# Down projection of a Strassen-like FFN: activation sums formed by the producer, w_down resident, last stores through GpSimd

## The chip, the cores and the metric

The kernel runs on one core of one Trainium2 chip. The metric is the device time in microseconds (us), median over several executions. A core has the engines TensorE (PE, matrix products; its weight loads are PEld), VectorE (DVE), ScalarE (ACT), GpSimd (POOL) and SyncE (SP, which here only issues DMAs). ACT and POOL can issue DMAs too. Each engine works through its own queue in order and waits on semaphores for the others.

## The reference, cut to what matters

One layer of an encoder on 1280 tokens (256 of a prompt, 1024 of a sample), model width 1024. The attention part is not touched by the change. The FFN is, with 2816 hidden columns:

```python
h2 = rmsnorm(x, ffn_norm_g)
x = x + (jax.nn.silu(h2 @ w_gate) * (h2 @ w_up)) @ w_down
return rmsnorm(x, final_norm_g)
```

All is float32.

## The kernel before

**Products.** A float32 product is made of three matmuls on operands split in a high and a low half: high x high, high x low, low x high (`mm3`, L104 to L107). The high half is a cast on ACT, the low half a subtraction on DVE or POOL.

**Seven products instead of eight.** Tokens fall in two halves T of 640, the hidden and output columns in two halves too, and each 2x2 block product is made of 7 products m of sums of blocks, in the order `SEQ2` = 3, 6, 1, 5, 2, 4, 7. Product 3 and product 4 take one block of the activations as they are; the other five take a sum or a difference of two.

**Gate and up.** A loop over 11 tile pairs fp (L950 on) makes gate (i = 0) and up (i = 1) for two tiles of 128 hidden columns: per product 2 x 12 matmuls of 128x320. POOL makes the sums of weight blocks (L866) and the low halves of the weights (L870), ACT the high halves (L869). Results are added from PSUM into the blocks `z` or `zB` (buffers of 2) by DVE (L930, L932), the first of them copied by ACT (L927). `finish` (L934 on) takes Silu of gate, multiplies up with it (L940, DVE) and stores the block of 320 KB to DRAM (`act_d`), on ACT's queue. Pair 0 is made in another order, while the sums S of the normalised input are still being made and split (L834 to L844).

**Down projection.** 77 steps (m, f), 7 products of 11 steps. A step takes one activation operand (128x640) and one operand of w_down (128x512), 15 matmuls of 128x512: five token tiles of 128, three each, into five PSUM banks `d`. `act_operand` (L1024 on) loads blocks back from DRAM, keeps them, and makes the sum of two (L1031; DVE for product 1, else POOL); `w_operand` (L1042 on) loads one or two tiles of w_down for every step and lets POOL add them (L1049). `split_f` makes the halves (ACT L1021, DVE L1022), in `ah` (3 buffers) and `wA` or `wB` (2 and 3). After the last step of a product, `put` (L1060 on) adds each bank into one or two rows of the residual x5, on DVE (L1065, L1067): 10 additions for products with two targets. Product 4 is followed by the final norm of five rows (`final`), product 7 by that of the other five (`final_half`), with output buffers taken from old activation slots. Operands are fetched two steps ahead.

**The order of the work.** A scheduler with a timeline of its own sets the order on PE, DVE, ACT and POOL. SP is in program order: it issues the loads of the gate and up weights, then, of the down stage, per step the activation block, the tiles of w_down and a row of x5.

Of the kernel before, what the change touches and what calls it, by code (L numbers as in the profile page):

```python
# [18 lines left out]
P = 128  # L19
# [20 lines left out]
def encoder_trunk(ctx: ExitStack, tc: tile.TileContext, x_tm, x_T, g_attn, w_c, w_v, w_qk,  # L40
# [10 lines left out]
    act_d = [tc.dram_tile([P, NTOK], F32, name=f"act_d{f}") for f in range(NF)]  # L51
# [864 lines left out]
    def product(C, seen, w, m, s, bank=None):  # L916
# [6 lines left out]
        for fi, T, sign in M_OUT[m]:  # L923
# [78 lines left out]
    halves = l5b.tile([P, 5], F32, name="halves")

    def slot(f, dt):
        return home[f].tile([P, 2, NQ], dt, name=f"a{f}")

    def act_block(b, f):
        T, n = int(b[0]) - 1, f + NH * (int(b[1]) - 1)
        if n not in act:
            act[n] = (slot(n, F32), set())  # L1010
        t, have = act[n]
        if T not in have:
            load(t[:, T], act_d[n][:, T * NQ:(T + 1) * NQ])
            have.add(T)
        return t[:, T]

    def split_f(o, raw, early):
        if early:
            split_w(o[:, 0], o[:, 1], raw)
        else:  # L1020
            nc.scalar.copy(out=o[:, 0], in_=raw)  # L1021
            nc.vector.tensor_sub(out=o[:, 1], in0=raw, in1=o[:, 0])  # L1022

    def act_operand(m, f):  # L1024
        src = [act_block(b, f) for b in A_OP[m] if isinstance(b, str)]
# [6 lines left out]
        if m == 7 and f >= NH - NLAST:  # L1032
            h = slot(f - (NH - NLAST), F32R)
        else:
            h = r5a.tile([P, 2, NQ], F32R, name="ah", bufs=3)
        split_f(h, raw, m == 3 and f == 0)
        return h

    nw = [0]

    def w_operand(m, f):
        raw = l5a.tile([P, 2, 512], F32, name="wd", bufs=3)  # L1042
        bs = [b for b in B_OP[m] if isinstance(b, str)]
        at = [f + NH * (int(b[0]) - 1) + NF * (int(b[1]) - 1) for b in bs]
        lo, n = min(at), len(at)
        load(raw[:, 0:n], w_down[lo:max(at) + 1:max(max(at) - lo, 1)].rearrange("n p d -> p n d"))
# [4 lines left out]
        if m == 7 and f == NH - 1:  # L1051
            w = slot(NH - 1, F32R)[:, :, 0:512]
        else:
            pl, nm, nb = (l5a, "wA", 2) if nw[0] % 5 < 2 else (l5b, "wB", 3)
            w = pl.tile([P, 2, 512], F32R, name=nm, bufs=nb)
        nw[0] += 1
        split_f(w, raw[:, 0], m == 3 and f == 0)
# [190 lines left out]
```

## Time and profile before

| | us |
|---|---|
| median of 3 runs | 1691.48 (1691.11 to 1692.06) |
| the profiled execution, device time | 1691.29 |
| its span in the profile | 1689.5 |
| PE busy | 1612.1 (95%) |
| DVE busy | 934.8 (55%) |
| POOL busy | 860.5 (51%) |
| ACT busy | 752.0 (45%) |

The span is the time from the first to the last instruction that the profile shows. The gate and up stage lies at about 837 to 1383.5 us (pair 0 to 896), the down projection from there to 1681.6. Shares are means over the span, so the table has to be read stage by stage. The granted TensorE clock is 0.991 of full speed in the mean.

### The profile page before, as it was taken

The page shows a single profiled execution, that of the slowest core. Times are in us where ns is not written, and L with a number is a line of the kernel's source. Part 1 is how long each engine was busy: PE and PEld are TensorE (multiplying, and loading weights), DVE is VectorE, ACT ScalarE, POOL GpSimd, SP SyncE. Part 2 cuts the span into 40 slices and gives each one's busy share as a digit, 9 for nine tenths or more (in the row PEclk, how much of TensorE's full clock was granted, in tenths as well). Part 3 has the DMA queues.
Part 4 walks back from the last instruction along what each step waited for, and adds up shares of the span by engine and source line. Part 5 has one row for each costly group of instructions (what it writes and reads, how often), then busy time and mean ns, then how long its engine had stood idle before and what let it go on. Part 6 is the DMA issues. An engine that isn't in the chain of part 4 may idle for free.

```text
span 1689.5 us, 26000 instructions
## 1 busy us (share of the span) xinstructions
PE 1612.1 (95%) x9601; PEld 1447.1 (86%) x9601; DVE 934.8 (55%) x1540; ACT 752.0 (45%) x1563; POOL 860.5 (51%) x914
## 2 busy tenths in 40 slices
PE   7999999998899999999989999999999999888998
PEld 7887899987798888888879999999999997666886
DVE  5753044545677677435583444443344447999665
ACT  5433154544677777534453333333333333233443
POOL 3441434353011119235386766666676666987344
PEclk9999999999999999999999999999999999999999
DMA  6635202143001012334241222121122249753354
GB/s 230 202 108 141 58 24 59 35 147 110 29 12 32 22 54 73 97 113 138 100 134 41 82 82 81 57 81 59 50 81 82 81 139 328 250 177 122 112 148 177
DMA packets 128144, 175.20 MB, mean 104 GB/s; under 512 B 35216, under 2 KB 66832, under 8 KB 128016
## 3 DMA queue, kind: packets, MB, share of 16 engines
q1 hardware_dynamic: 88080, 135.18, 25.1%
q10 hardware_dynamic: 39936, 38.35, 6.7%
q8 instruction: 76, 1.25, 0.3%
q14 instruction: 52, 0.43, 0.1%
HBM read 133.84 MB, written 39.65 MB: 103 GB/s over the span
## 4 chain that ended last, share of the span: by engine, by line
PE 75%; DVE 6%; issue 6%; DMA 5%; POOL 5%; ACT 3%; SPq 0%; ACTq 0%; POOLq 0%; DVEq 0%
PE M L107 10%; PE M L106 10%; PE M L105 10%; PE o L681 3%; PE tp L674 3%; PE d L107 3%; PE d L105 3%; PE d L106 3%; PE na_o L457 2%; PE po L105 2%; PE pj L105 2%; PE po L106 2%; PE po L107 2%; PE pj L107 2%; PE pj L106 2%
## 5 line engine op out<-in xcount | busy, mean ns | idle before, releaser
L105 PE MATMUL M<-S,wc 128*128 128x320 f32 x1056 | 325.9, 309 | 2.9 <-ACT wc L869 2.5
L107 PE MATMUL M<-S,wc 128*128 128x320 f32 x1056 | 324.5, 309 | 4.1 <-POOL wc L870 4.1
L106 PE MATMUL M<-S,wc 128*128 128x320 f32 x1056 | 326.4, 309 | 2.1 <-DVE S L840 2.0
L870 POOL TENSOR_TENSOR wc<-sum,wc 128x512 fp32r<-128x512 f32 x110 | 150.6, 1370 | 113.6 <-ACT wc L869 113.6
L105 PEld LDWEIGHTS M<-S,wc 128*128 128x128 f32 x1056 | 198.1, 188 | 4.2 <-ACT wc L869 3.2
L107 PEld LDWEIGHTS M<-S,wc 128*128 128x128 f32 x1056 | 197.6, 188 | 4.6 <-POOL wc L870 4.6
L106 PEld LDWEIGHTS M<-S,wc 128*128 128x128 f32 x1056 | 198.1, 188 | 3.2 <-DVE S L840 3.1
L866 POOL TENSOR_TENSOR sum<-A,A 128x512 f32<-128x512 f32 x110 | 159.1, 1455 | 9.4 <-DMA A<-in_w_gate_dram 3.1
L869 ACT CAST wc<-sum 128x512 fp32r<-128x512 f32 x110 | 68.3, 621 | 213.0 <-PE M L106 173.1
L930 DVE TENSOR_TENSOR z<-M,z 128x320 f32<-128x320 f32 x144 | 67.8, 486 | 118.2 <-PE M L107 84.5
L1049 POOL TENSOR_TENSOR wd<-wd 128x512 f32<-128x512 f32 x55 | 84.8, 1543 | 75.7 <-DMA wd<-in_w_down_dram 60.4
L930 DVE TENSOR_TENSOR zB<-M,zB 128x320 f32<-128x320 f32 x120 | 56.8, 487 | 108.5 <-PE M L107 74.7
L96 DVE TENSOR_TENSOR PT<-tp,PT 128x512 fp32r<-128x512 f32 (+1 forms) x144 | 93.0, 657 | 40.3 <-ACT PT L95 38.9
L694 POOL TENSOR_TENSOR ob<-ob 128x128 f32<-128x128 f32 x40 | 18.3, 457 | 180.0 <-ACT ob L691 179.9
L95 ACT CAST PT<-tp 128x512 fp32r<-128x512 f32 (+1 forms) x144 | 79.1, 564 | 44.0 <-PE tp L674 41.0
L666 DVE TENSOR_REDUCE mm<-S 128x1 f32<-128x1024 f32 (+1 forms) x80 | 84.9, 1061 | 14.1 <-PE S L107 12.6
L107 PE MATMUL d<-wB,ah 128*128 128x512 f32 x210 | 79.1, 406 | 9.8 <-DVE ah L1022 9.8
L870 POOL TENSOR_TENSOR wc<-A,wc 128x512 fp32r<-128x512 f32 x44 | 65.1, 1481 | 45.3 <-ACT wc L869 45.3
L106 PE MATMUL d<-wB,ah 128*128 128x512 f32 x210 | 83.9, 403 | 1.6 <-DVE wB L1022 1.6
L674 PE MATMUL tp<-ident,ex 128*128 128x128 f32 x544 | 79.7, 274 | 4.8 <-ACT ex L668 3.5
L105 PE MATMUL d<-wB,ah 128*128 128x512 f32 x210 | 83.6, 401 | 0.1
L681 PE MATMUL o<-PT,v 128*128 128x256 f32 x544 | 81.5, 288 | 1.6 <-ACT PT L95 1.4
(418 smaller groups left out, 4311.4 us busy)
## 6 DMA issues: line engine op xcount, KB each, us to landing
wd<-in_w_down_dram SPq DMA_DIRECT2D x55, 512.0 KB
a<-act_d SPq DMA_DIRECT2D x44, 320.0 KB
A<-in_w_gate_dram SPq DMA_DIRECT2D x52, 256.0 KB
A<-in_w_up_dram SPq DMA_DIRECT2D x52, 256.0 KB
x<-in_x_tm_dram SPq DMA_DIRECT2D x20, 512.0 KB
act_d<-z ACTq DMA_DIRECT2D x24, 320.0 KB
cT_d<-stg ACTq DMA_DIRECT2D x20, 320.0 KB
act_d<-zB ACTq DMA_DIRECT2D x20, 320.0 KB
```

Source lines behind the costliest of these rows:

```text
L95: i = nc.scalar.copy(out=hi, in_=ps)
L96: nc.vector.tensor_sub(out=lo, in0=ps, in1=hi)
L105: nc.tensor.matmul(out, lhsT=sh, rhs=mh, start=first, stop=False)
L106: nc.tensor.matmul(out, lhsT=sh, rhs=ml, start=False, stop=False)
L107: nc.tensor.matmul(out, lhsT=sl, rhs=mh, start=False, stop=last)
L666: nc.vector.reduce_max(out=nm[:, u:u + 1], in_=S, axis=AX.X, negate=True)
L674: nc.tensor.transpose(tp[:, j], ex[:, kt * P:(kt + 1) * P], ident)
L681: nc.tensor.matmul(oT, lhsT=vv, rhs=pt[s][g][:, j], start=kt == 0 and s == 0, stop=kt == nkt - 1 and s == 1)
L866: nc.gpsimd.tensor_tensor(out=raw, in0=A[a], in1=A[b], op=op)
L870: i1 = nc.gpsimd.tensor_tensor(out=lo, in0=raw, in1=hi, op=ALU.subtract)
L930: nc.vector.tensor_add(out=o, in0=ps, in1=o)
L1049: nc.gpsimd.tensor_tensor(out=raw[:, 0], in0=raw[:, i], in1=raw[:, 1 - i], op=B_OP[m][1])
```

## The change

`finish` now makes all seven activation operands of the pair while its blocks are in SBUF: two are blocks as they are, five are sums made by DVE (L964 of the new kernel), put over gate's old blocks or, for product 5, over a block of up. It stores seven arrays of 320 KB per pair instead of four, on ACT's queue, those of the last pair on POOL's (`store_p`). The down stage loads one ready array per step (`as`, 4 buffers). Each tile of w_down is loaded once, 11 times 512 KB and 22 times 256 KB, and stays in SBUF (`w0_f`, `w1_f`); DVE adds two of them where a product wants a sum (`ws`, L1065 of the new kernel, 2 buffers). The halves of a step go to `ah` and `w` (5 buffers each), loads are issued four steps ahead, and the output rows of `final` have 2 buffers. One early load of constants is issued after four memsets instead of before them.

```diff
+    def store_p(out, in_):
+        nc.gpsimd.dma_start(out=out, in_=in_)
...
     def finish(G, U, which, m, fp):
...
                 nc.vector.tensor_mul(out=U[:, fi, cs], in0=U[:, fi, cs], in1=G[:, fi, cs])
-                store(act_d[2 * fp + fi][:, cs], U[:, fi, cs])
+        if which == 0:
+            return
...
+        for n in AFTER.get(m, ()):
+            src = [block(U, b) for b in ACT_OP[n] if isinstance(b, str)]
+            out = src[0]
+            if len(src) == 2:
+                out = block(G, INTO[n]) if n in INTO else src[1]
+                nc.vector.tensor_tensor(out=out, in0=src[0], in1=src[1], op=ACT_OP[n][1])
+            (store_p if fp == NF // 2 - 1 else store)(act_d[n][fp], out)
...
-            if m in (1, 6):
-                raw = r5a.tile([P, NQ], F32, name="as", bufs=2)
-            eng = nc.vector if m == 1 else nc.gpsimd
-            eng.tensor_tensor(out=raw, in0=src[0], in1=src[1], op=A_OP[m][1])
...
+    def load_a(m, f):
+        araw[m, f] = r5b.tile([P, NQ], F32, name="as", bufs=4)
+        load(araw[m, f], act_d[m][f])
+
     def act_operand(m, f):
...
+        h = r5b.tile([P, 2, NQ], F32R, name="ah", bufs=5)
+        split_f(h, araw.pop((m, f)))
+        return h
+
+    def w_operand(m, f):
+        src = [wraw[b, f] for b in B_OP[m] if isinstance(b, str)]
         raw = src[0]
         if len(src) == 2:
...
-        if n == 2:
-            i = at.index(lo)
-            nc.gpsimd.tensor_tensor(out=raw[:, 0], in0=raw[:, i], in1=raw[:, 1 - i],
-                                    op=B_OP[m][1])
...
+            raw = r5b.tile([P, 512], F32, name="ws", bufs=2)
+            nc.vector.tensor_tensor(out=raw, in0=src[0], in1=src[1], op=B_OP[m][1])
+        w = l5w.tile([P, 2, 512], F32R, name="w", bufs=5)
+        split_f(w, raw)
         return w
...
-        yo = slot(NLAST + n % 5, F32).rearrange("p a b -> p (a b)")[:, 0:D]
...
+        yo = r5a.tile([P, D], F32, name="yo", bufs=2)
...
-    AHEAD = 2
+    AHEAD, LOADED = 2, 4
...
+    for step in steps[:LOADED]:
+        bring(*step)
     for step in steps[:AHEAD]:
         fetch(*step)
     for i, (m, f) in enumerate(steps):
+        if i + LOADED < len(steps):
+            bring(*steps[i + LOADED])
         if i + AHEAD < len(steps):
             fetch(*steps[i + AHEAD])
```

The order moves at three places. First DVE's queue where gate/up hands over to the down projection. Before (M0, M1 are gate/up products in PSUM, z_14403 and z_14402 up and gate of the last pair, `ah`, `wA`, `wB` halves of the down stage's operands):

```order
L930 TENSOR_TENSOR z_14403<-M0_14890,z_14403 128x320
L930 TENSOR_TENSOR z_14403<-M1_14904,z_14403 128x320
L940 TENSOR_TENSOR z_14403<-z_14403,z_14402 128x640
L1022 TENSOR_TENSOR ah_14969<-a1_14967,ah_14969 128x640
L1022 TENSOR_TENSOR wA_14975<-wd_14972,wA_14975 128x512
L1022 TENSOR_TENSOR ah_14980<-a2_14978,ah_14980 128x640
```

And now, at the same place (z_14538 and z_14537 are up and gate, L964 the activation sums, L1065 the sums of w, L1029 the low halves):

```order
L934 TENSOR_TENSOR z_14538<-M1_15041,z_14538 128x320
L1065 TENSOR_TENSOR ws_15116<-w1_0_15093 128x512
L951 TENSOR_TENSOR z_14538<-z_14538,z_14537 128x640
L1029 TENSOR_TENSOR w_15118<-ws_15116,w_15118 128x512
L964 TENSOR_TENSOR z_14537<-z_14538 128x640 x2
L964 TENSOR_TENSOR z_14538<-z_14538 128x640
L1029 TENSOR_TENSOR ah_15113<-as_15095,ah_15113 128x640
L1065 TENSOR_TENSOR ws_15124<-w1_1_15097 128x512
L1029 TENSOR_TENSOR ah_15121<-as_15099,ah_15121 128x640
L1065 TENSOR_TENSOR ws_15138<-w1_2_15101 128x512
L1029 TENSOR_TENSOR w_15126<-ws_15124,w_15126 128x512
L1029 TENSOR_TENSOR w_15140<-ws_15138,w_15140 128x512
```

A w sum now stands before the last product with gate, and three activation sums stand before the first low half of an activation; the halves of step 0 were made on POOL before and are not in DVE's queue there.

The second place is SP's queue from the first load of the down stage on. Before (`a` activation blocks, `wd` tiles of w_down, `x5` rows of the residual):

```order
L63 DMA a0_14956<-act_d0_62 128x640
L63 DMA wd_14961<-in_w_down_dram 128x2x512
L63 DMA a1_14967<-act_d1_63 128x640
L63 DMA wd_14972<-in_w_down_dram 128x2x512
L63 DMA a2_14978<-act_d2_64 128x640
L63 DMA wd_14983<-in_w_down_dram 128x2x512
L63 DMA x5_14989<-xm_d0_84 128x512
L63 DMA a3_15011<-act_d3_65 128x640
L63 DMA wd_15016<-in_w_down_dram 128x2x512
```

And now:

```order
L64 DMA w1_0_15093<-in_w_down_dram 128x2x512
L64 DMA as_15095<-act3_d0_84 128x640
L64 DMA w1_1_15097<-in_w_down_dram 128x2x512
L64 DMA as_15099<-act3_d1_85 128x640
L64 DMA w1_2_15101<-in_w_down_dram 128x2x512
L64 DMA as_15103<-act3_d2_86 128x640
L64 DMA x5_15105<-xm_d0_139 128x512
L64 DMA w1_3_15107<-in_w_down_dram 128x2x512
L64 DMA as_15109<-act3_d3_87 128x640
```

The row x5_15105 lies where the gate and up blocks were, so its load waits for the last pair's stores, which POOL issues now; the tile of w_down for step 3 is queued behind it.

The third place is DVE's queue at the end of product 3 (`d_...` are the PSUM banks, L1065 before and L1075 now the additions of `put`). Before:

```order
L1022 TENSOR_TENSOR ah_15240<-as_15238,ah_15240 128x640
L1022 TENSOR_TENSOR wA_15246<-wd_15243,wA_15246 128x512
L1022 TENSOR_TENSOR wB_15273<-wd_15270,wB_15273 128x512
L1065 TENSOR_TENSOR x5_14989<-d_14991,x5_14989 128x512
L1065 TENSOR_TENSOR x5_15134<-d_14991,x5_15134 128x512
L1022 TENSOR_TENSOR ah_15267<-as_15265,ah_15267 128x640
L1065 TENSOR_TENSOR x5_15022<-d_14992,x5_15022 128x512
```

And now:

```order
L1065 TENSOR_TENSOR ws_15429<-w0_1_15366,w1_1_15097 128x512
L1029 TENSOR_TENSOR ah_15398<-as_15341,ah_15398 128x640
L1075 TENSOR_TENSOR x5_15105<-d_15143,x5_15105 128x512
L1075 TENSOR_TENSOR x5_15225<-d_15143,x5_15225 128x512
...
L1065 TENSOR_TENSOR ws_15467<-w0_2_15393,w1_2_15101 128x512
L1029 TENSOR_TENSOR ah_15426<-as_15368,ah_15426 128x640
L1075 TENSOR_TENSOR x5_15167<-d_15146,x5_15167 128x512
...
L1075 TENSOR_TENSOR x5_15314<-d_15147,x5_15314 128x512
L1029 TENSOR_TENSOR w_15431<-ws_15429,w_15431 128x512
```

Before, both halves of w for the second step of product 6 (wB_15273) were made ahead of the additions; now its low half (w_15431) stands behind all ten.

## Rows read from the trace of the kernel before

**Rows 1.** Page: span; busy time, share of it and instructions of each engine.
```profile
span 1689.5 us, 26000 instructions
...
PE 1612.1 (95%) x9601; PEld 1447.1 (86%) x9601; DVE 934.8 (55%) x1540; ACT 752.0 (45%) x1563; POOL 860.5 (51%) x914
```

**Rows 2.** Stages: stretch, length, then PE, PEld, DVE, ACT, POOL busy, clock, DMA share, GB/s.
```profile
837.00:896.00 59.00, 48.88 (x318) 46.25 (x318) 47.58 (x59) 30.45 (x47) 45.44 (x27) 1.00 0.31 102
896.00:1383.50 487.50, 487.50 (x3327) 487.50 (x3327) 196.16 (x359) 170.65 (x332) 329.67 (x240) 1.00 0.21 72
1383.50:1430.00 46.50, 46.50 (x200) 36.72 (x199) 29.77 (x34) 16.85 (x27) 27.12 (x19) 1.00 0.93 338
1430.00:1550.00 120.00, 100.09 (x395) 73.60 (x394) 115.88 (x87) 36.83 (x58) 106.04 (x57) 0.97 0.57 195
1550.00:1681.60 131.60, 131.60 (x566) 105.92 (x564) 89.25 (x113) 56.83 (x100) 50.73 (x49) 1.00 0.44 138
```

**Rows 3.** PE in order of time: start, us, line, operation, tile.
```profile
1383.36 0.31 PE L107 MATMUL M<-zA,wc 128*128 128x320 f32 x1
1383.51 1.32 PE L105 MATMUL d<-wA,ah 128*128 128x512 f32 x5
...
1560.00 0.40 PE L105 MATMUL d<-wB,ah 128*128 128x512 f32 x1
...
1566.77 0.40 PE L107 MATMUL d<-wB,ah 128*128 128x512 f32 x1
...
1681.40 0.40 PE L107 MATMUL d<-a,a 128*128 128x512 f32 x1
```

**Rows 4.** Two stretches of 5 us, columns as in rows 2.
```profile
845.00:850.00 5.00, 2.73 (x15) 2.24 (x16) 2.82 (x4) 3.23 (x5) 5.00 (x4) 1.00 0.42 128
...
1470.00:1475.00 5.00, 3.89 (x11) 2.45 (x11) 5.00 (x4) 1.68 (x3) 5.00 (x4) 0.61 0.08 9
```

**Rows 5.** Waits, 1375 to 1690: who waits for whom, us, times, longest.
```profile
PEld d L107 <- DVE ah L1022: 26.9, 21, 2.6
```

**Rows 6.** DVE's groups by form, 1384 to 1410: count, busy us, mean ns, idle before.
```profile
L1022 DVE TENSOR_TENSOR ah<-a,ah 128x640 fp32r<-128x640 f32 x8 | 7.7, 958 | 3.0 <-ACT ah L1021 3.0
L1022 DVE TENSOR_TENSOR wB<-wd,wB 128x512 fp32r<-128x512 f32 x5 | 3.5, 691 | 7.8 <-ACT wB L1021 7.8
```

**Rows 7.** The same, 1440 to 1550.
```profile
L1022 DVE TENSOR_TENSOR ah<-as,ah 128x640 fp32r<-128x640 f32 x17 | 29.8, 1753 | 0.2 <-ACT ah L1021 0.2
...
L1065 DVE TENSOR_TENSOR x<-d,x 128x512 f32<-128x512 f32 x15 | 9.4, 675 | 0.0
```

**Rows 8.** POOL's groups by form, 1440 to 1550.
```profile
L1031 POOL TENSOR_TENSOR a<-a,a 128x640 f32<-128x640 f32 x22 | 44.9, 2041 | 4.9 <-DMA a<-act_d 4.8
L1049 POOL TENSOR_TENSOR wd<-wd 128x512 f32<-128x512 f32 x16 | 28.3, 1766 | 3.5 <-DMA wd<-in_w_down_dram 1.5 <-DVE as L1031 0.7 <-DVE wA L1022 0.7
```

**Rows 9.** DVE in order of time at the handover.
```profile
1384.23 0.82 DVE L940 TENSOR_TENSOR z<-z 128x640 f32<-128x640 f32 x1
1386.22 0.83 DVE L1022 TENSOR_TENSOR ah<-a,ah 128x640 fp32r<-128x640 f32 x1 [1.16 <-ACT ah L1021]
1386.96 0.68 DVE L1022 TENSOR_TENSOR wA<-wd,wA 128x512 fp32r<-128x512 f32 x1
```

**Rows 10.** Chain that ended last, 1375 to 1410: start, us, what.
```profile
1382.51 2.96 DMA act_d<-z
...
1386.45 5.03 DMA wd<-in_w_down_dram
```

**Rows 11.** DVE's groups by form, 1555 to 1660.
```profile
L1022 DVE TENSOR_TENSOR ah<-a,ah 128x640 fp32r<-128x640 f32 x29 | 28.2, 971 | 24.6 <-ACT ah L1021 24.6
...
L1076 DVE SCALAR_TENSOR_TENSOR a<-x,ry,gl_b 128x1024 f32<-128x1024 f32 x5 | 6.3, 1272 | 0.0
```

**Rows 12.** Weight loads in order of time, tile pair 0.
```profile
888.24 0.19 PEld L107 LDWEIGHTS M<-S,wc 128*128 128x128 f32 x1 [2.30 <-POOL wc L870]
```

**Rows 13.** DVE's and POOL's groups by form, 896 to 1383.
```profile
L940 DVE TENSOR_TENSOR z<-z 128x640 f32<-128x640 f32 x20 | 25.5, 1275 | 0.8
L866 POOL TENSOR_TENSOR sum<-A,A 128x512 f32<-128x512 f32 x97 | 133.8, 1388 | 5.5 <-POOL wc L870 0.8
```

More of the change, by code (lines that the diff above doesn't have):

```diff
@@ L50, in encoder_trunk @@
     rope_d = tc.dram_tile([2, 2, P, NTOK], F32R, name="rope_d")
-    act_d = [tc.dram_tile([P, NTOK], F32, name=f"act_d{f}") for f in range(NF)]
+    act_d = {m: [tc.dram_tile([P, NTOK // 2], F32, name=f"act{m}_d{f}") for f in range(NF // 2)]
+             for m in range(1, 8)}
     xm_d = [tc.dram_tile([P, D], F32, name=f"xm_d{t}") for t in range(NT)]
@@ L372, in encoder_trunk @@
             nc.gpsimd.memset(z[64 - 64 * hh:128 - 64 * hh].bitcast(F32), 0.0)
+    load(mp_s, m_prompt)
     def na_bias(p):
@@ L932, in product @@
                 nc.vector.tensor_sub(out=o, in0=o, in1=ps)
+    ACT_OP = {3: ("11",), 4: ("22",), 2: ("21", ALU.add, "22"), 7: ("12", ALU.subtract, "22"),
+              1: ("11", ALU.add, "22"), 6: ("21", ALU.subtract, "11"),
+              5: ("11", ALU.add, "12")}
+    AFTER = {2: (4, 2), 4: (7,), 7: (3, 1, 6, 5)}
+    INTO = {2: "21", 7: "12", 1: "22", 6: "11"}
     def finish(G, U, which, m, fp):
@@ L940, in finish, with block @@
                 nc.vector.tensor_mul(out=U[:, fi, cs], in0=U[:, fi, cs], in1=G[:, fi, cs])
-                store(act_d[2 * fp + fi][:, cs], U[:, fi, cs])
+        if which == 0:
+            return
+        def block(X, b):
+            T, fi = int(b[0]) - 1, int(b[1]) - 1
+            return X[:, fi, T * NQ:(T + 1) * NQ]
+        for n in AFTER.get(m, ()):
[5 more added lines that the diff above has]
+            (store_p if fp == NF // 2 - 1 else store)(act_d[n][fp], out)
     last = last + w31[1, 1][2:]
@@ L995, in encoder_trunk @@
     NLAST = 5
-    l5a, l5x, l5b = l5 = [pool("l5a"), pool("l5x"), pool("l5b")]
-    r5a, r5b, r5c, r5d = r5 = [pool(nm, side="right") for nm in ("r5a", "r5b", "r5c", "r5d")]
+    l5w, l5x, l5r = l5 = [pool("l5w"), pool("l5x"), pool("l5r")]
+    r5a, r5b = r5 = [pool(nm, side="right") for nm in ("r5a", "r5b")]
     pd = pool("pd", space=PSUM)
-    home = {f: r5c if f < 4 else r5d if f < 8 else l5b if f < 11 or f > 19 else r5b for f in range(NF)}
-    act, xs, ssy = {}, {}, {}
-    gl_b = l5b.tile([P, D], F32, name="gl_b")
@@ L1002, in encoder_trunk @@
[L1002 to L1022, printed above, removed]
@@ L1024, in act_operand, with split_f, load_w @@
-    def act_operand(m, f):
-        src = [act_block(b, f) for b in A_OP[m] if isinstance(b, str)]
+    xs, wraw = {}, {}
+    gl_b = r5a.tile([P, D], F32, name="gl_b")
+    halves = r5a.tile([P, 5], F32, name="halves")
+    def split_f(o, raw):
+        nc.scalar.copy(out=o[:, 0], in_=raw)
+        nc.vector.tensor_sub(out=o[:, 1], in0=raw, in1=o[:, 0])
+    def load_w(m, f):
+        bs = [b for b in B_OP[m] if isinstance(b, str) and (b, f) not in wraw]
+        if not bs:
+            return
+        dh = int(bs[0][1]) - 1
+        if ("t", dh, f) not in wraw:
+            pl = l5r if dh == 1 and f < NH - 1 else r5a
+            wraw["t", dh, f] = pl.tile([P, 2, 512], F32, name=f"w{dh}_{f}")
+        t = wraw["t", dh, f]
+        ks = sorted(int(b[0]) - 1 for b in bs if int(b[1]) - 1 == dh)
+        at = 2 * f + NF * dh
+        load(t[:, ks[0]:ks[-1] + 1],
+             w_down[at + ks[0]:at + ks[-1] + 1].rearrange("n p d -> p n d"))
+        for k in ks:
+            wraw[f"{k + 1}{dh + 1}", f] = t[:, k]
+        load_w(m, f)
@@ L1030, in act_operand @@
-            eng = nc.vector if m == 1 else nc.gpsimd
-            eng.tensor_tensor(out=raw, in0=src[0], in1=src[1], op=A_OP[m][1])
[L1032 to L1046, printed above, removed]
-        if n == 2:
-            i = at.index(lo)
-            nc.gpsimd.tensor_tensor(out=raw[:, 0], in0=raw[:, i], in1=raw[:, 1 - i],
-                                    op=B_OP[m][1])
[L1051 to L1057, printed above, removed]
@@ L1070, in final @@
         x = xs[n]
-        yo = slot(NLAST + n % 5, F32).rearrange("p a b -> p (a b)")[:, 0:D]
-        ss = l5b.tile([P, 1], F32, name="ssy", bufs=3)
-        r = l5b.tile([P, 1], F32, name="ry", bufs=3)
+        yo = r5a.tile([P, D], F32, name="yo", bufs=2)
+        ss = r5a.tile([P, 1], F32, name="ssy", bufs=3)
+        r = r5a.tile([P, 1], F32, name="ry", bufs=3)
         nc.scalar.activation(yo, x, AF.Square, accum_out=ss)
@@ L1087, in final_half @@
         x, half = xs[n], halves[:, n:n + 1]
-        yo = slot(NLAST + n % 5, F32).rearrange("p a b -> p (a b)")[:, 0:D]
-        ss = l5b.tile([P, 1], F32, name="ssy", bufs=3)
-        r = l5b.tile([P, 1], F32, name="ry", bufs=3)
+        yo = l5r.tile([P, 2, 512], F32, name=f"w1_{n}").rearrange("p a b -> p (a b)")
+        ss = r5a.tile([P, 1], F32, name="ssy", bufs=3)
+        r = r5a.tile([P, 1], F32, name="ry", bufs=3)
         nc.scalar.activation(yo[:, 0:512], x[:, 0:512], AF.Square, accum_out=ss)
@@ L1108, in fetch, with bring @@
         ops[m, f] = act_operand(m, f), w_operand(m, f)
+    def bring(m, f):
+        load_w(m, f)
+        load_a(m, f)
         for n in (f - 2,) if 2 <= f < NH - 1 else (NT - 2, NT - 1) if f == NH - 1 else ():
```

2 lines of the change are left out of this document (1 added, 1 removed).

## The prediction

> **What bounds the kernel now.** I read the page's busy times first, then a table of the span by stage, then the matmuls' pitch, then the waits of the slow stage, and last what VectorE (DVE) and GpSimd (POOL) do in it. TensorE (PE) is busy 95% of the span [rows 1], but that is an average over stages. In the gate/up stage after tile pair 0 (896 to 1383.5) PE is busy all 487.5 us: nothing can be gained there, only lost. In the down stage it is full from 1383.5 to 1430, busy 100.1 of 120 us from 1430 to 1550, full again to 1681.6, and the span ends at 1689.5, 7.9 us later [rows 1, 2].
>
> How much is lost in the down stage follows from the pitch. Between 1560.00 and 1566.77 there are 29 matmuls of 128x512 without a pause, 6.77/29 = 0.2334 us each. The stage has 7 products x 11 steps x 15 = 1155 of them, 1155 x 0.2334 = 269.6 us. It runs from 1383.51 to 1681.63 (the last one begins at 1681.40) [rows 3], 298.1 us. So 28.5 us are lost. The outer stretches are worth 46.5/0.2334 = 199 and 131.6/0.2334 = 564 matmuls, which leaves 392 in the middle, 91.5 us of work in 120 us: all 28.5 us are lost there. 19.9 of them are gaps; the rest is slow matmuls, among them 5 us at a mean granted clock of 0.61, so partly at 1.2 instead of 2.4 GHz, behind the gaps [rows 4].
>
> What PE waits for there is DVE's low half of the activation operand (26.9 us on the weight loads alone) [rows 5]. DVE is busy 115.9 of the 120 us and POOL 106.0 [rows 2]. Yet DVE's work is not long in itself: the low half of `ah` takes 958 ns and that of `wB` 691 from 1384 to 1410 [rows 6], and 1753 ns from 1440 to 1550 [rows 7], when POOL runs sums of 2041 and 1766 ns next to each other [rows 8]. PSUM additions, with one operand in SBUF, stay at 675 ns [rows 7]. So the two engines hold each other up where both read two SBUF operands, and PE pays. DMA load isn't it: DVE is at its short durations while DMA is at 0.93 share before 1430, and slow at 0.57.
>
> **The change part by part, down stage.** All of POOL's sums in this stage go; POOL is left with a few tiny operations and 5 multiplies. DVE gets the sums of w. Per step it then does a w sum, the low half of w (0.6 to 0.7 us each by the length at 1386.96 [rows 9]) and the low half of the activation (0.74 to 0.83 by spacing and length at 1386.22 [rows 9]), about 2.0 us; 60 additions from PSUM of 0.68 [rows 7] over 77 steps add 0.5. That is 2.6 us against PE's 15 x 0.2334 = 3.50 us per step, so PE sets the pace: I take back the whole 28.5 us, and then count what the new order gives away. Loads are no limit on average: in the first product 832 KB per step and 256 KB of x5 in 3.5 us are 311 GB/s, and 338 were moved over the stretch to 1430 with PE full [rows 2].
>
> *Handover.* Call T the end of the last gate/up matmul, 1383.36 + 0.31 = 1383.67 [rows 3]. Before, the first down operand was ready early (built by POOL) and PE went on without a gap. Now DVE's queue has the first w sum behind the last addition from PSUM, and then the product with gate, the low half of w, and three of the five activation sums, and only then the first activation's low half. By the durations there [rows 9]: addition done T+0.53 (the next operation starts at 1384.23); w sum T+1.14; ScalarE's high half T+1.8; product T+1.96; low half of w T+2.6; three sums (0.7 to 0.8) T+4.7; low half of the activation T+5.45. PE's first ten matmuls of step 0 fit before, the last five run from 5.45 to 6.7. Step 1: DVE does w sum (6.1), low half (6.8), w sum 2 (7.4), low half of w (8.0); the five first matmuls run from 6.7, the other ten from 8.0 to 10.4. Step 2 is ready by then and ends T+13.9. Three steps alone need 10.5: 3.4 us lost.
>
> *The stores through POOL.* The first x5 load stands in SP's queue behind nothing but waits for the last pair's stores (its space is the old gate and up tiles), and w1_3 stands behind it. The last of those stores is issued at about T+3.9. No store by POOL is in these rows; the nearest is ScalarE's of the same block, 2.96 us from issue to landing, and for the loads after it 5.03 us for 512 KB [rows 10]. With 4.7 us for the store, x5_0 goes at T+8.6, w1_3 lands near T+12.8, its sum, high half and first matmuls are at T+14.9 instead of 13.9: 1.0 us. With the 2.96 of the row it is 0; with a store twice as slow, 5 us more (rival 1).
>
> *First boundary.* At the end of product 3 each of 5 banks is added into two places, 10 additions, and in DVE's queue the low half of w for product 6, step 1 stands behind all ten, with a w sum and an activation's low half among them. The first bank is done 4 x 0.2334 = 0.93 us before the product's end: -0.93 + 10 x 0.61 (0.68 less an overlap as at 1386.22) + 0.65 + 0.75 + 0.65 gives 7.2 us after that end; PE, with step 0 and the first third of step 1 to do, comes to it at 3.5 + 1.17 = 4.67. 2.6 us lost. At the five other boundaries three steps (10.5 us) are prepared in front of the additions: 0.
>
> *Last product.* Output rows have 2 buffers instead of 5, so ScalarE's square waits for a store two rows back and holds the high halves queued behind it. The final row costs DVE 1272 ns and ScalarE about as much [rows 11]. By my count the operand of step 8 is ready at 24.5 us into the product, needed at 24.7: between 0 and 3, I take 0.5. The tail after the last matmul stays at 7.9 us.
>
> *Gate/up.* Five sums and three more stores per tile pair go on DVE and ScalarE, 11 times. In pair 0, DVE is the late one already (busy 47.6 of 59 us with PE at 48.9 [rows 2], and a weight load that waits 2.30 us for POOL's low half [rows 12]); one new sum of 0.82 stands ahead of the S7 split: 0.8, at most 3 sums, 2.5. In the ten others, operands are made three products ahead; POOL is 329.7/487.5 = 68% busy, DVE 40% [rows 2]: 0, with the cover being POOL's 16 us of idle time per pair of 48.9 us. The DVE product of the same shape takes 1275 ns there against 825 alone, because of POOL [rows 9, 13]. The extra 0.45 us is what meeting an operation of 1388 ns in 68% of cases would cost on average (0.68 x 0.69 = 0.47). The Trainium skill says of this (SBUF — State Buffer, "Who interferes with whom") that a DVE instruction with two SBUF inputs and a GpSimd instruction that reads SBUF exclude each other for a whole instruction, whoever starts first; the trace agrees by that 0.45. Blocked POOL time is then 5 x 0.83 = 4.2 us per pair, inside 16.
>
> Moving one early load behind four memsets changes no engine's order: 0.
>
> **Sum.** 1691.3 (the profiled execution: span 1689.5 and 1.8 around it, 0.2 under the median of 1691.48) - 28.5 + 3.4 + 1.0 + 2.6 + 0.5 + 0.8 = 1671.1. Nothing given away would be 1662.8. The same stalls could bring the lower clock back: 5 us at 0.61 cost 0.39 x 5 = 2 us, while a stretch with PE busy 2.73 of 5 us left it at 1.00 [rows 4]; I count none. Likeliest case alone: 1667 to 1677.
>
> **Rivals.**
> 1. *The stores through POOL are held up* while DVE works without pause at the handover. For it: DVE has about 13 us of queue with hardly a gap there, and both engines hold each other up in this trace. Against it: no store by POOL is shown. Price: x5_0 only when DVE first pauses, near T+13, w1_3 usable at T+19 instead of 14: 5 us, 1676. The Trainium skill has such a rule (SBUF — State Buffer, "SBUF: two separate sides"): GpSimd can't write a DMA's descriptors while VectorE holds the shared port. No row here shows it.
> 2. *DVE itself becomes the bound.* If its operations stay nearer the 971 ns that `ah` has from 1555 to 1660 [rows 11], each boundary stalls like the first: 5 x 2.6 = 13 more, 1684. Against it: in that stretch POOL still ran 50.7 of 131.6 us [rows 2]. With a stall in the last product on top, 1688 to 1691, no change.
> 3. *Slower: gate/up pays.* PE has no slack there. ScalarE issues the stores in order, behind the sums that they wait for, and makes the high halves of the weights. If that, with POOL blocked, makes PE wait over 20.2/11 = 1.8 us per pair, the gain is gone; two of the five sums uncovered, each with a blocked POOL operation (2 x 1.27), are 2.5 us x 11 = 28: 1699. Against it: PE waits nowhere there now, with operands six halves ahead.
>
> **How the numbers follow.** Likeliest 0.55; rival 1 0.13; rival 2 0.12, and its no-change form 0.05; rival 3 0.08; less given away (1663 to 1667) 0.07. Range 1664 to 1684. A measurement of this kernel tells about 0.2%, 3.4 us, from no change. Faster 0.55 + 0.13 + 0.12 + 0.07 = 0.87, same 0.05, slower 0.08.
>
> **What would show it.** In the profile after: 1430 to 1550 with PE above 95%, `ah` low halves near 0.8 us and POOL nearly idle; a gap of 3 to 5 us in the first 15 us of the down stage, PE waiting for DVE and then for w1_3; one near 2.6 us after product 3 and no other of its size; gate/up after pair 0 still 487.5 us. Wrong if `ah` stays at 1.7 us with POOL silent, if gate/up is longer by more than 5 us, or if PE waits at every boundary.

## The result and the profile after

The changed kernel takes 1668.97 us (median of 4 runs, 1667.90 to 1670.22) against 1691.77 us for the kernel before (4 runs). The ratio is 0.9864, with a 95% interval from 0.9847 to 0.9881: 1.4% faster. The forecast was 1671 us.

The page of the changed kernel, span and busy times:

```profile
span 1667.8 us, 26037 instructions
...
PE 1607.0 (96%) x9601; PEld 1450.4 (87%) x9601; DVE 950.5 (57%) x1641; ACT 751.4 (45%) x1565; POOL 689.2 (41%) x818
```

PE and DVE do about what they did before [rows 1]; POOL lost 171 us. A share of the span says little about where that helped, so next come the stages, with the same columns as [rows 2] (length, busy PE, PEld, DVE, ACT, POOL, clock, DMA share, GB/s):

```profile
837.00:896.00 59.00, 52.08 (x331) 49.76 (x330) 51.06 (x58) 29.65 (x45) 49.03 (x28) 0.97 0.33 110
896.00:1379.50 483.50, 483.50 (x3299) 483.27 (x3297) 249.16 (x407) 169.96 (x332) 318.88 (x235) 1.00 0.25 89
1379.50:1430.00 50.50, 44.37 (x186) 34.42 (x185) 35.90 (x54) 19.04 (x30) 2.53 (x5) 1.00 0.92 342
1430.00:1550.00 120.00, 119.05 (x502) 95.73 (x503) 78.98 (x117) 45.88 (x78) 5.25 (x5) 0.99 0.40 127
1550.00:1659.60 109.60, 109.60 (x470) 88.19 (x468) 78.28 (x112) 45.21 (x77) 11.79 (x21) 1.00 0.42 135
```

The stretch from 1430 to 1550, with PE busy 100.1 us before, is nearly full (119.05). POOL is silent there, and DVE fell from 115.9 to 79.0 us although it took the w sums over. In exchange the first 50 us of the down stage are no longer full: 44.4 of 50.5. The gate/up stage stayed full with 53 us more work on DVE.

PE in order of time, the starts behind a gap of the down stage, the last gate/up matmul and the last matmul of all (start, us, line, operation, tile, idle before and who ended it):

```profile
1379.23 0.31 PE L111 MATMUL M<-zA,wc 128*128 128x320 f32 x1
1381.99 0.50 PE L109 MATMUL d<-w,ah 128*128 128x512 f32 x1 [2.46 <-ACT ah L1028]
...
1385.03 1.43 PE L111 MATMUL d<-w,ah 128*128 128x512 f32 x5 [0.43 <-DVE ah L1029]
...
1395.40 1.44 PE L109 MATMUL d<-w,ah 128*128 128x512 f32 x5 [1.71 <-ACT ah L1028]
...
1430.95 0.50 PE L110 MATMUL d<-w,ah 128*128 128x512 f32 x1 [2.48 <-DVE w L1029]
...
1659.59 0.40 PE L111 MATMUL d<-w,ah 128*128 128x512 f32 x1
```

These four are the only gaps over 0.25 us in the 77 steps; before there were 20. I use one measure from here on: from the start of the last gate/up matmul to the start of the last down matmul. It was 1681.40 - 1383.36 = 298.04 us [rows 3] and is 1659.59 - 1379.23 = 280.36 us. The whole difference of the two profiled executions (spans 1689.51 and 1667.78, 21.73 us) is put together from the start times of single matmuls, which stand in the same order in both:

| stretch | before | after | difference | forecast |
|---|---|---|---|---|
| up to the first gate/up matmul | 800.94 | 798.10 | -2.84 | 0 |
| tile pair 0 (336 matmuls) | 90.20 | 88.90 | -1.30 | +0.8 |
| tile pairs 1 to 10 | 492.53 | 492.53 | 0.00 | 0 |
| down stage, measured as above | 298.04 | 280.36 | -17.68 | -21.0 |
| from the last matmul's start to the end | 8.11 | 8.19 | +0.08 | 0 |

(The rows overlap by one matmul of 0.31 us, the same in both. A few of pair 0's matmuls run from 800.94 us on, among the end of the attention part, ahead of the stretch that begins at 837 in [rows 2].) Down the seven products, start to start: before 38.7, 44.8, 54.2, 45.0, 38.5, 38.5 and 38.2 us; after 41.6, 42.9 and then 38.66 four times and 38.4. All that was lost before lay in products 6, 1 and 5; what is lost now lies in products 3 and 6.

Of the forecast's own tests: DVE's groups from 1440 to 1550, to be read beside [rows 7] (count, busy us, mean ns, idle before).

```profile
L1029 DVE TENSOR_TENSOR ah<-as,ah 128x640 fp32r<-128x640 f32 x31 | 26.5, 855 | 34.7 <-ACT ah L1028 34.7
L1075 DVE TENSOR_TENSOR x<-d,x 128x512 f32<-128x512 f32 x20 | 12.9, 683 | 3.2 <-PE d L111 3.2
L1029 DVE TENSOR_TENSOR w<-ws,w 128x512 fp32r<-128x512 f32 x16 | 11.0, 685 | 0.1
...
L1065 DVE TENSOR_TENSOR ws<-w,w 128x512 f32<-128x512 f32 x15 | 10.4, 691 | 0.8 <-DMA w<-in_w_down_dram 0.4
```

The low half of the activation went from 1753 to 855 ns, the addition from PSUM stayed (675, 683). POOL is busy 5.25 us of the 120 from 1430 to 1550, PE 99%. No product behind product 6 loses anything, so rival 2 (DVE as the bound) falls too.

### The profile page after: what moved, and what is told of

Same layout as the page of the kernel before. It is cut to its first block, busy times and chain, and to the rows that moved or that the text cites. A ratio compares the mean times of both kernels' runs of the same rounds, so it can differ in the third digit from the quotient of the medians.

```text
span 1667.8 us, 26037 instructions
## 1 busy us (share of the span) xinstructions
PE 1607.0 (96%) x9601; PEld 1450.4 (87%) x9601; DVE 950.5 (57%) x1641; ACT 751.4 (45%) x1565; POOL 689.2 (41%) x818
## 4 chain that ended last, share of the span: by engine, by line
PE 84%; issue 4%; DMA 4%; POOL 3%; ACT 2%; DVE 2%; SPq 0%; POOLq 0%; ACTq 0%; DVEq 0%
PE M L111 10%; PE M L110 10%; PE M L109 10%; PE d L110 5%; PE d L109 5%; PE d L111 5%; PE o L685 3%; PE tp L678 3%; PE na_o L461 2%; PE po L109 2%; PE pj L109 2%; PE pj L111 2%; PE pj L110 2%; PE po L110 2%; PE po L111 2%
## 5 line engine op out<-in xcount | busy, mean ns | idle before, releaser
L110 PE MATMUL d<-w,ah 128*128 128x512 f32 x385 | 147.4, 398 | 2.5 <-DVE w L1029 2.5
L109 PE MATMUL d<-w,ah 128*128 128x512 f32 x385 | 144.5, 400 | 4.2 <-ACT ah L1028 4.2
L111 PE MATMUL d<-w,ah 128*128 128x512 f32 x385 | 145.4, 398 | 0.4 <-DVE ah L1029 0.4
L1028 ACT CAST ah<-as 128x640 fp32r<-128x640 f32 x77 | 56.0, 727 | 121.7 <-issue 71.3
L109 PEld LDWEIGHTS d<-w,ah 128*128 128x128 f32 x385 | 73.1, 190 | 22.8 <-ACT ah L1028 5.0
L1029 DVE TENSOR_TENSOR ah<-as,ah 128x640 fp32r<-128x640 f32 x77 | 64.1, 836 | 50.4 <-ACT ah L1028 50.4
L110 PEld LDWEIGHTS d<-w,ah 128*128 128x128 f32 x385 | 72.7, 189 | 20.7 <-DVE w L1029 3.2
```

The source lines that it names most:

```text
L109: nc.tensor.matmul(out, lhsT=sh, rhs=mh, start=first, stop=False)
L110: nc.tensor.matmul(out, lhsT=sh, rhs=ml, start=False, stop=False)
L111: nc.tensor.matmul(out, lhsT=sl, rhs=mh, start=False, stop=last)
```

## The experiments

Medians are compared only within a group that shared a chip. The changed kernel's own median was 1668.97 us in one group and 1672.52 in another; in the profiled runs of the two 2.65 us of that lie ahead of gate/up, where short drops of the clock come and go (point 1 of the next section). So the down stage in the trace, as measured above, is the sharper number; it stands beside each.

### What held VectorE up

**GpSimd busy with additions that nobody needs.**

```diff
     def fetch(m, f):
         ops[m, f] = act_operand(m, f), w_operand(m, f)
+        if m in (6, 1, 5):
+            t = wraw["t", 0, f]
+            for _ in range(2):
+                nc.gpsimd.tensor_tensor(out=pj, in0=t[:, 0], in1=t[:, 0], op=ALU.add)
```

> The new kernel with two GpSimd additions of 128x512 per step of products 6, 1 and 5 (66 in all), whose result nobody reads. Theory (the two engines hold each other up where both read two SBUF operands, and that was the loss before): VectorE's low halves in that stretch go from 0.69 and 0.85 us to 1.3 us or more, its work per step from 2.6 to over 3.5 us, TensorE waits again, 10 to 25 us slower than the new kernel: 1679 to 1694, I say 1684. Rival (the loss before came from the length of the operand chain through GpSimd, not from GpSimd being busy): within 2 us of the new kernel, 1667 to 1671.

Measured: 1689.59 us (10 runs), ratio to the kernel before 0.9985 [0.9970, 0.9999]; down stage 296.7 us. Of the 17.7 us gained there, 1.4 are left.

**The control: GpSimd busy with memsets.**

```diff
+        if m in (6, 1, 5):
+            t = wraw["t", 0, f]
+            if (m, f) == (6, 0):
+                nc.gpsimd.tensor_tensor(out=pj, in0=t[:, 0], in1=t[:, 0], op=ALU.add)
+            for _ in range(6):
+                nc.gpsimd.memset(pj, 0.0)
```

> The control of the run with additions: GpSimd is busy for as long in the same products, but with memsets of 128x512, which read nothing (198 of them, result unread). Theory, in the form that only reading counts: VectorE's low halves stay at 0.69 and 0.85 us, 1667 to 1671. Rival (any GpSimd work in SBUF holds VectorE up): as slow as with additions, 1679 or more.

Measured: 1668.50 us, ratio 0.9867 [0.9843, 0.9892]; down stage 280.7 us.

**The kernel before, its sums moved to VectorE and nothing else.**

```diff
-            eng = nc.vector if m == 1 else nc.gpsimd
+            eng = nc.vector
...
-            nc.gpsimd.tensor_tensor(out=raw[:, 0], in0=raw[:, i], in1=raw[:, 1 - i],
+            nc.vector.tensor_tensor(out=raw[:, 0], in0=raw[:, i], in1=raw[:, 1 - i],
```

> The kernel before with one thing changed: the sums of activations and of w_down in the down stage are made by VectorE instead of GpSimd (the first step's halves stay on GpSimd). w_down is still loaded again and again, the activation sums are still made in the down stage, the handover is as before. Theory: VectorE then has up to 4 operations per step in product 1, 6 and 7 (2.85 us and 0.5 of additions, under TensorE's 3.50), low halves at 0.7 to 0.85 us, and 15 to 25 us of the 28.5 come back: 1667 to 1677, I say 1671. Rival (the gain comes from the sums moved to the producer and from the resident w_down): less than 8 us come back, 1684 or more, since VectorE is late by itself.

Measured: 1672.51 us, ratio 0.9887 [0.9867, 0.9907]; down stage 277.6 us, 2.8 us shorter than that of the changed kernel. The handover did not stay as before: the first w sum, now DVE's, comes behind the last product with gate, and PE waits 2.75 us for the halves that POOL makes of it.

**The w sums of the changed kernel on GpSimd.**

```diff
-            nc.vector.tensor_tensor(out=raw, in0=src[0], in1=src[1], op=B_OP[m][1])
+            nc.gpsimd.tensor_tensor(out=raw, in0=src[0], in1=src[1], op=B_OP[m][1])
```

> The new kernel with the sums of w_down on GpSimd instead of VectorE, all else as it is. Theory: 55 GpSimd additions meet VectorE's two subtractions per step; VectorE's work falls to 1.4 us plus 0.5 per step and grows by its waits to under 3.5, so TensorE mostly keeps its pace, with low halves near 1.1 us: 1668 to 1675. Rival (it is GpSimd in the chain that costs, at whatever load): 1680 or more.

Measured: 1671.56 us, ratio 0.9879 [0.9857, 0.9901]; down stage 281.3 us.

The same 100 us in five kernels (1440 to 1540, within products 6, 1 and 5; columns as in the stages above). Before:

```profile
1440.00:1540.00 100.00, 83.69 (x329) 61.50 (x327) 95.88 (x71) 30.78 (x48) 91.92 (x49) 0.97 0.56 189
```

After:

```profile
1440.00:1540.00 100.00, 100.00 (x428) 80.46 (x428) 60.26 (x89) 36.24 (x59) 0.00 (x0) 1.00 0.37 117
```

With GpSimd adding:

```profile
1440.00:1540.00 100.00, 89.81 (x369) 70.67 (x368) 97.16 (x88) 32.61 (x53) 73.64 (x53) 0.95 0.38 119
```

With GpSimd writing:

```profile
1440.00:1540.00 100.00, 100.00 (x428) 80.41 (x427) 63.27 (x95) 37.37 (x61) 88.60 (x169) 1.00 0.42 131
```

The kernel before with its sums on VectorE:

```profile
1440.00:1540.00 100.00, 97.52 (x417) 77.75 (x416) 95.44 (x141) 37.84 (x59) 0.00 (x0) 1.00 0.69 234
```

Read the third column (DVE) with its count and the fifth (POOL). With POOL adding, DVE is busy 97.2 us over 88 instructions; with POOL writing for even longer (88.6 us), DVE is busy 63.3 us over 95, as with POOL silent. In the last line DVE is as busy as in the first, but with 141 instructions instead of 71. Long DVE time alone is not work: its mean per instruction tells the two apart. The single durations say the same, with GpSimd adding (DVE by form, 1440 to 1540):

```profile
L1030 DVE TENSOR_TENSOR ah<-as,ah 128x640 fp32r<-128x640 f32 x27 | 35.7, 1322 | 2.4 <-ACT ah L1029 2.4
L1030 DVE TENSOR_TENSOR w<-ws,w 128x512 fp32r<-128x512 f32 x19 | 27.4, 1448 | 0.0
...
L1076 DVE TENSOR_TENSOR x<-d,x 128x512 f32<-128x512 f32 x15 | 9.4, 673 | 0.0
```

and with GpSimd writing:

```profile
L1030 DVE TENSOR_TENSOR ah<-as,ah 128x640 fp32r<-128x640 f32 x30 | 24.7, 823 | 32.9 <-ACT ah L1029 32.9
L1030 DVE TENSOR_TENSOR w<-ws,w 128x512 fp32r<-128x512 f32 x19 | 12.9, 685 | 0.1
...
L1076 DVE TENSOR_TENSOR x<-d,x 128x512 f32<-128x512 f32 x15 | 9.5, 682 | 3.2 <-PE d L111 3.2
```

Operations with two operands in SBUF take up to twice as long when POOL reads SBUF as well (823 to 1322 and 685 to 1448 ns); those with one operand in PSUM don't change; a POOL that only writes changes nothing. An operation on POOL that reads a single operand was not tried. The Trainium skill has this rule (SBUF — State Buffer, "Who interferes with whom"): a DVE instruction with two SBUF inputs contends with a GpSimd instruction that reads SBUF, "not with one that only writes it"; both halves of it agree with these rows.

So the theory stands and both rivals fall: the length of the operand chain isn't it, since nothing waits for the useless additions, and the resident w_down and the producer's sums aren't needed for the gain, since moving two sums to DVE in the old kernel takes 20.5 us off its down stage. With w sums alone on POOL, DVE meets POOL often (low half of w 1139 ns) but has slack, and PE keeps its pace: products 1 and after are as short as in the changed kernel; only product 3 is 3.5 us longer, and product 6 2.5 us shorter. In the trace's down stage the old kernel with its sums on DVE is ahead of the changed one, so the producer's sums and the resident w_down brought nothing more there.

### What the change gives away

**Additions after product 3 behind the low half of w.**

```diff
-                put(m, t, ps[t])
+                with ExitStack() as es:
+                    if m == 3:
+                        es.enter_context(tc.issue_after(wlo[6, 1].ins))
+                    put(m, t, ps[t])
```

(`wlo` holds the low-half instructions of w by step.)

> The new kernel with the additions after product 3 ordered behind the low half of w of product 6, step 1, on VectorE. Theory: the 2.5 us stall at this boundary goes, and the lower clock that follows it in the profile (some 1.5 us) with it: 3 to 4 us under the new kernel, 1664 to 1666, and the stretch from product 3 to product 6 without a gap. Rival (the stall only moves, since ten additions take VectorE's time wherever they stand): a gap of about the same size at step 2 or 3 of product 6, 1668 to 1670.

Measured: 1665.52 us, ratio 0.9848 [0.9827, 0.9868]. The gap at 1430.95 is gone and none came in its place: product 6 takes 38.65 us instead of 42.91, the down stage 276.2 us. That is 4.2 us, where 3 to 4 were expected. The stretch behind the start of product 6 in this run (columns as above; the same of the changed kernel stands in point 6 of the next section):

```profile
1427.00:1432.00 5.00, 5.00 (x23) 4.04 (x22) 5.00 (x9) 0.73 (x1) 0.00 (x0) 1.00 0.45 167
1432.00:1437.00 5.00, 5.00 (x23) 4.03 (x22) 5.00 (x9) 2.50 (x4) 0.00 (x0) 1.00 0.70 202
```

**Rows of x5 two steps later.**

```diff
-        for n in (f - 2,) if 2 <= f < NH - 1 else (NT - 2, NT - 1) if f == NH - 1 else ():
+        for n in (f - 4,) if 4 <= f < NH - 1 else range(NT - 4, NT) if f == NH - 1 else ():
```

> The new kernel with the loads of the x5 rows issued two steps later, so that the tiles of w_down for steps 3 and 4 don't stand behind the first of them in SyncE's queue. Theory: the wait of 1.9 us before step 3 goes, 1.5 to 2.5 us under the new kernel: 1666 to 1668. Rival (step 3 waits for the DMA engines, which the last pair's stores and the loads share, not for the queue's order): the wait stays, 1668 to 1670.

Measured: down stage 278.2 us, product 3 39.65 us instead of 41.63; step 3 starts 14.0 us after the last gate/up matmul, as steps 0 to 2 allow, instead of 15.9. In the trace the theory holds for the wait before step 3. The boundary to product 6 is no better: instead of one wait of 2.48 us there are three of 0.37, 1.19 and 1.72, the clock stays at 1.00 behind them, and product 6 takes 42.74 us (42.91). The median, 1670.61 us, ratio 0.9880 [0.9860, 0.9899], misses the 1666 to 1668 expected: 2 us are within the scatter of the runs.

**The last pair's stores on ScalarE's queue.**

```diff
-            (store_p if fp == NF // 2 - 1 else store)(act_d[n][fp], out)
+            store(act_d[n][fp], out)
```

> The new kernel with the last tile pair's seven stores on ScalarE's queue like those of the other pairs. Theory (it was ScalarE's in-order queue that the change spares): each store waits in ScalarE's queue for its sum on VectorE with the first high halves behind it; the last sum ends 3.9 us after the last gate/up matmul, so the first steps come 2 to 4 us later: 1671 to 1674, and the landings take 3 to 5 us. Rival (stores through GpSimd are held up by VectorE and cost more than this): faster than the new kernel, 1664 to 1667.

Measured: 1671.49 us, ratio 0.9879 [0.9859, 0.9898]; down stage 279.8 us. Of the expected delay of 2 to 4 us less came, and it did not last. Step 0 starts 3.2 us after the last gate/up matmul instead of 2.5, step 1 at 8.4 instead of 6.8 (part of that is the clock, which dropped behind the first gap here; in another run of the changed kernel where it did so too, step 1 starts at 7.6). But the wait before step 3 is gone, and step 4 starts at 18.9 instead of 19.5. ScalarE's queue (start, us, idle before and its end; ACTq are the issues of the stores) shows the casts between the stores:

```profile
1383.64 0.62 ACT L1028 CAST w<-ws 128x512 fp32r<-128x512 f32 x1 [7.73 <-DMA act_d<-z]
1384.49 0.33 ACTq L67 DMA_DIRECT2D act_d<-z  x1
1384.94 0.73 ACT L1028 CAST ah<-as 128x640 fp32r<-128x640 f32 x1 [0.68 <-DMA as<-act_d]
1386.02 2.61 ACTq L67 DMA_DIRECT2D act_d<-z  x3
1388.75 0.72 ACT L1028 CAST ah<-as 128x640 fp32r<-128x640 f32 x1 [3.09 <-DMA act_d<-z]
```

So the last pair's stores through POOL are worth nothing here within what this can tell: they spare ScalarE and pay as much at the x5 row.

**The two orderings together.** The diff is that of both.

> The two orderings that worked in the trace together: x5 rows later (2.0 us in product 3) and the low half of w before the additions (4.3 us at the boundary). Theory (they add up): down stage 280.4 - 2.0 - 4.2 = 274.2 us, 1663 to 1665, a ratio of 0.983 to 0.985. Rival (with x5 rows later, the additions after product 3 wait for the last four rows, as a gap of 1.6 us at product 6 showed): 275.5 to 276.5 us, no better than the low half alone.

Measured: 1668.80 us, ratio 0.9860 [0.9840, 0.9879]; down stage 274.8 us. They add up in the trace to within 0.6 us (274.2 expected), and that much the clock costs here, which dropped behind the handover's gap (step 3 starts at 14.6 instead of 14.0); the rival's 275.5 doesn't come. The median misses the 1663 to 1665 expected, and the ratio the 0.983 to 0.985.

**With the handover's order as well.**

```diff
+    for a, b in [(s, wlo[3, 1].ins) for s in late_sums] + [(last_put[0], alo[3, 0].ins), (last_put[0], wlo[3, 0].ins)]:
+        tc.add_manual_dep(a, b.name, ...)
```

(a is issued behind b; `late_sums` are the three activation sums after the last product, `last_put` the last addition of gate/up, `wlo` and `alo` the low halves by step.)

> Three edits together, for a version that beats both: the two orderings (x5 rows later, low half of w before the additions) and, at the handover, VectorE's first w sum and the low halves of step 0 ordered before the last addition of gate/up, the activation sums of the last pair behind step 1's operands. Theory: of the handover's 3.5 us at least 2 go, of the wait before step 3 1.9, of the boundary 2.5 and its clock 1.5: the down stage falls from 280 to 271 to 274 us, 1660 to 1663. Rival (the first operands aren't there before the last gate/up matmul, or the late sums push the stores and x5 rows onto the path): the handover keeps its gap, 1664 to 1667.

Measured: 1666.28 us, ratio 0.9852 [0.9834, 0.9870]; down stage 274.4 us. The handover's gap fell from 2.46 to 1.91 us only: the first w sum still waits for a gate/up matmul, the rival's reason, and the median is the rival's too (1664 to 1667), not the 1660 to 1663 expected. Step 1 starts at 5.9 instead of 6.8, step 4 at 17.5, as with the late x5 rows alone. The run was made again beside the changed kernel:

> The combination with the handover's order, once more, beside the one without it. Theory from its first trace: at the handover it wins 0.9 us up to step 1 and gives them back at steps 2 and 3, where sums and stores come late; down stage 274.4 us, the same as the two orderings alone within 0.5 us, ratio 0.983 to 0.985. Rival (the handover's order is worth its full 2 us): 1 to 2 us under the two orderings alone.

> The new kernel unchanged, on the same chip as the two combinations, so that differences of 0.2 to 0.4% can be told from the chip and from the clock drops ahead of the FFN, which move single runs by 2 to 4 us. Theory: down stage 280 to 282 us, a ratio to the kernel before of 0.985 to 0.989.

Measured on one chip: the changed kernel 1672.52 us, ratio 0.9883 [0.9861, 0.9904], down stage 280.1; the two orderings 1668.80; the three edits 1666.93 us, ratio 0.9858 [0.9838, 0.9877], down stage 275.2. The handover's order is worth nothing more in the down stage (275.2 against 274.8). Its median is 1.9 us under that of the two orderings, as the rival had it, but the profiled runs differ by more ahead of the change: gate/up begins at 798.89 us in one and 804.13 in the other. These two versions beat the changed kernel by 3.7 and 5.6 us in the medians and by 5 in the down stage, though the intervals of the ratios overlap.

## Why the prediction was right, and where it was not

The reason was right and is shown: DVE and POOL held each other up, the stall was 28.5 us long, and it is gone with POOL's reads. The time came out within 2 us, but partly by luck: the down stage lost 3.3 us more than forecast, and pair 0 (2.1 us better than forecast) and the 2.8 us ahead of the change, which the change did not make, more than covered that. By its own steps:

1. **What lies ahead of the change: 0, measured -2.8.** Not an effect of the change. The granted clock drops from 2.4 to 1.2 GHz for some microseconds at places ahead of gate/up, and which of them appear differs from run to run: the kernel before had drops of 3.4 us at 153.6 and 426.6 us that the changed one had not, while the instructions there are the same. Over these two places the changed kernel gains 1.6 and 1.7 us; small differences elsewhere run the other way. The first gate/up matmul starts anywhere from 797.98 to 804.13 us in the 13 traces, and the times of single runs scatter with it.

2. **Pair 0: +0.8, measured -1.3.** The sign was wrong. All eleven traces with the new kernel's gate/up took 88.87 to 89.31 us for it, some with a clock drop inside; the old order took 90.20 without one and 91.83 with two (the kernel before with its sums on VectorE). So it is hardly chance, though the old order has two traces only. The step that failed is that the new sum ahead of the S7 split would show: up to matmul 288 both take 79.8 us, and the 1.3 lie in the last 48. In before, a low half of the last weights on POOL cost a weight load 2.30 us [rows 12] and PE 2.04; after, PE's wait at that place is 0.25 us, and one just before it 1.00 instead of 0.54. The scheduler put POOL's and DVE's work in another order there; which swap is worth it was not tried.

3. **Gate/up pairs 1 to 10: 0, measured 0.00.** 492.53 us, the same in every run of the new kernel's order. The new sums cost DVE what the product did, held up by POOL (896 to 1379, by form):

```profile
L964 DVE TENSOR_TENSOR zB<-zB 128x640 f32<-128x640 f32 x25 | 29.6, 1212 | 0.2
L964 DVE TENSOR_TENSOR z<-z 128x640 f32<-128x640 f32 x24 | 29.1, 1240 | 0.1
L951 DVE TENSOR_TENSOR zB<-zB 128x640 f32<-128x640 f32 x20 | 25.8, 1290 | 0.7
```

PE never noticed. That ends rival 3.

4. **Handover: 3.4, measured 3.5.** DVE in order of time:

```profile
1379.57 0.49 DVE L934 TENSOR_TENSOR z<-M,z 128x320 f32<-128x320 f32 x1 [0.54 <-PE M L111]
1379.98 0.68 DVE L1065 TENSOR_TENSOR ws<-w 128x512 f32<-128x512 f32 x1
...
1381.95 2.29 DVE L964 TENSOR_TENSOR z<-z 128x640 f32<-128x640 f32 x3
1384.16 0.82 DVE L1029 TENSOR_TENSOR ah<-as,ah 128x640 fp32r<-128x640 f32 x1
...
1388.23 0.82 DVE L1029 TENSOR_TENSOR ah<-as,ah 128x640 fp32r<-128x640 f32 x1
1393.38 0.69 DVE L1065 TENSOR_TENSOR ws<-w 128x512 f32<-128x512 f32 x1 [4.32 <-DMA w<-in_w_down_dram]
```

With T = 1379.54 the first low half of an activation ends at T+5.44 (forecast 5.45), and steps 1, 2 and the end of step 2 follow at T+6.8, 10.5 and 14.0 (forecast 6.7, 10.4, 13.9).

5. **The x5 row behind the stores: 1.0, measured 1.9.** The mechanism holds. POOL's last two stores, and SP's queue:

```profile
1383.80 0.54 POOL L70 DMA_DIRECT2D act_d<-z  x1 [0.20 <-issue]
1384.54 0.54 POOL L70 DMA_DIRECT2D act_d<-z  x1 [0.20 <-issue]
```

```profile
1375.52 0.47 SPq L64 DMA_DIRECT2D as<-act_d  x1
1388.79 0.33 SPq L64 DMA_DIRECT2D x<-xm_d  x1
1389.16 0.43 SPq L64 DMA_DIRECT2D w<-in_w_down_dram  x1
```

SP stands still for 13 us and goes on 0.15 us after the landing of the first of these two at 1388.64, 4.84 us after its issue (4.7 were assumed). Each link came a little later: the row at T+9.25 instead of 8.6, the w sum at T+13.8, and PE had to wait for ScalarE's second cast too, which I had left out. The size varies: in four other traces with this order the wait before step 3 cost 1.0, 1.5, 1.7 and 2.0 us. Rival 1 fails on the same rows: DVE has no gap of note from 1379.98 to 1389.05, and three stores were issued and landed within that time (landings at 1387.01, 1387.83 and 1388.64). That holds for the additions and subtractions that DVE did here; other operations were not tried.

6. **First boundary: 2.6, measured 2.48 and 1.7 on top.** The wait has the size forecast. The step that failed is "I count none" of the clock:

```profile
1425.00:1430.00 5.00, 3.47 (x15) 2.45 (x13) 5.00 (x9) 1.25 (x2) 0.00 (x0) 1.00 0.29 91
1430.00:1435.00 5.00, 4.05 (x12) 3.21 (x13) 5.00 (x9) 1.39 (x3) 0.00 (x0) 0.74 0.77 253
1435.00:1440.00 5.00, 5.00 (x21) 4.03 (x20) 4.97 (x9) 2.23 (x4) 0.00 (x0) 0.92 0.98 339
```

Behind the gap the clock is at 1.2 instead of 2.4 GHz for 3.4 us. The same drop stands there in each of the four traces that keep this wait at 2.5 us, and in none of those that shortened it or, as with the late x5 rows, split it. Taking the wait away gave 4.2 us back, not 2.5. The gap of 2.46 us at the handover had such a drop in some runs and in others not.

7. **Last product: 0.5, measured 0** (38.4 us). And a term that I had not seen: a matmul of the down stage now takes 0.2343 us from start to start instead of 0.2331 in the same products (38.66 and 38.46 us per product). Over 1155 that is 1.4 us. It is even over all 15 positions of a step, and the old kernel with its sums on VectorE has the old pitch; the cause is open.

Together, by the forecast's pitch of 0.2334: 3.5 + 1.9 + 2.5 + 1.7 + 1.0 = 10.6 us given away in the down stage, where 7.5 were forecast; 10.8 are measured (280.36 - 269.6). One sum of the forecast is a little off without harm: the loads of the first product are 318 GB/s and not 311, since its KB have 1024 bytes, still under the 338 that were moved.

## What to carry to other kernels

When two engines are both near 100% busy in a stage, compare the mean duration of one instruction there with the same instruction elsewhere before counting work: here about half of DVE's time in its operations on two SBUF operands was waiting for POOL (1753 ns against 855), and giving all the work to one of them was faster than sharing it. The collision was shown for sums and differences of two SBUF operands on DVE beside sums on POOL; additions from PSUM and pure writes stayed out of it, so a sum on GpSimd should be cheap beside those and is dear beside other sums once DVE has no slack. A gap in a full TensorE stage can cost more than its length, since the clock can drop behind it (2.5 us cost 4.2 here): order the next product's operands ahead of the last one's additions.

## What was not expected of the hardware

- 198 memsets on GpSimd (527 ns each) beside VectorE cost nothing, 66 additions (1368 ns each) cost 16 us of the down stage.
- A drop of the clock for 3.4 us costs 1.7 us where PE is full (behind product 3, at 153.6 and at 426.6 us) and can cost nothing elsewhere: pair 0 took 88.90 us in the changed kernel's first trace, with such a drop at 845.3 us, and 88.99 in its second, without one. Two more or fewer of them ahead of the change are as large as most of what was tried here.
- The pitch of the same matmul is 234.3 against 233.1 ns in the two kernels; no run shows why.
